# A wider first piece for a pooling kernel: 1500 columns on partitions 0 to 74 instead of 840 on 0 to 29

## Chip, cores, metric

One core of one Trainium2 chip. The metric is the device time of one execution in microseconds (us). Every execution is listed with its span too, the time from the first to the last instruction in the trace; for the kernel before the device time is 1.74 to 1.83 us longer than the span. All executions here are of the fast state with a granted clock of 1.00, but for one kernel that ran only once, whose state is unknown for that reason.

Terms: DVE is the vector engine, ACT the scalar engine, SBUF the on-chip memory of 128 partitions. A load or store is spread over up to 16 DMA engines, which move it in packets, here one per row (what one partition holds of it). An engine that has done its share sends an increment to a semaphore; at the sixteenth the transfer has landed.

## The reference

```python
# x: (32, 256, 4096) float32, p = 2, kernel_size = 4
for i in range(out_length):                       # 1024
    window = np.abs(x[:, :, 4*i:4*i+4]) ** p
    result[:, :, i] = np.mean(window, axis=-1) ** (1.0 / p)
```

So each four neighbours give the square root of the mean of their squares. 134.22 MB are read and 33.55 MB written; nothing is reused.

## The kernel before

The input is taken as one flat array, seen as 128 partitions by 262,144 columns. 20 loads of up to 13,184 columns go through three buffers. ACT squares a load in place, DVE sums the fours, ACT takes the root, and the result is stored. Loads are issued from the sync queue, most stores from ACT's. Ahead of the first load comes a small "first piece" of the array's end, in another shape: 840 columns of the 128-partition view, laid on 30 partitions.

```python
    slots += [[(W, [5792, 7392])], [(10808, [6592, 2808, 1408])]]   # the last load
    ODD = 840
    ...
    Q = 30
    odd = ODD * P // Q                                  # 3584 columns on 30 partitions
    t = o_tiles[1][0:Q, 0:odd]
    nc.sync.dma_start(out=t, in_=xf[(total - ODD) * P:total * P].rearrange("(p w) -> p w", p=Q))
    ahead = 0
    while ahead < n and loads[ahead][0] < X_SLOTS:      # the first three loads
        load(ahead)
        ahead += 1
    nc.vector.tensor_tensor(out=t, in0=t, in1=t, op=mybir.AluOpType.mult)
    ...                                                 # reduce, root
    stores["odd"] = nc.scalar.dma_start(...)            # 30 rows of 896
    for i in range(n):                                  # the 20 loads
        ...                                             # load ahead, square, sum, root, store
    for g in sorted(late):
        store(g, nc.sync)                               # the last four stores
```

What the first piece is for: a transfer of 30 rows runs on 15 DMA engines, one of 128 rows on 16. So one engine has no part in the first piece and gets a little less to do than the others. Below it is called **the engine outside**, and the others **the 15**.

## Time and profile before

| | kernel before |
|---|---|
| device time at first, median of 3 executions | 393.83 us (393.81 to 395.14) |
| the same with all 6 executions of the first comparison | 394.30 us (393.63 to 395.37) |
| span of the profiled execution | 393.33 us |
| moved by the DMA engines | 167.77 MB, 427 GB/s over the span |
| DVE, ACT busy | 70%, 70% |

The lines are from the timeline of the profiled execution (start us, duration us, engine, line, operation, shapes, and in brackets the idle time of the engine before it and what ended it):

```profile
4.96 3.88 DVE L137 TENSOR_TENSOR ot<-ot 30x3584 f32<-30x3584 f32 x1 [4.96 <-DMA ot<-in_x_dram]
20.60 11.19 ACT L167 ACTIVATE xt<-xt 128x13184 f32<-128x13184 f32 x1 [6.87 <-DMA xt<-in_x_dram]
```

They serve as clocks for two landings: DVE can begin when the first piece has landed on its last engine (4.96 us), and ACT when the first load has (20.60 us).

### The profile page before, as it was taken

To read this page: it belongs to the slowest core of one execution; us is meant where nothing else is said; L and a number is where in the kernel's file an instruction comes from. 1 tells how busy PE (TensorE), PEld (TensorE's weight loads), DVE (VectorE), ACT (ScalarE), POOL (GpSimd) and SP (SyncE) were. 2 spreads that over 40 slices of the span, in tenths; PEclk is the share of its full clock that TensorE was granted. 3 is DMA by queue.
4 is the path that set the end of the run, shared out by engine and by line. 5 is a ranking of instruction groups with operands and counts; after the bars stand their busy time and mean duration, and the time that the engine had idled before them with its cause. 6 is when DMAs were issued, how large, how long until landed. Compare 5 with 4: busy or idle time off the path is not lost.

```text
span 393.3 us, 182 instructions
## 1 busy us (share of the span) xinstructions
DVE 274.5 (70%) x36; ACT 275.4 (70%) x38; POOL 0.2 (0%) x4
## 2 busy tenths in 40 slices
DVE  4207898885869376948693869396929690989991
ACT  1095879919990899099809991998099809986991
POOL 0000000000000000000000000000000000000000
DMA  8999999999989999999999999999999899999996
GB/s 312 429 440 429 467 445 451 381 432 469 434 386 429 472 429 429 456 402 429 429 432 426 429 472 429 456 400 467 429 437 429 386 429 467 429 429 423 440 409 295
DMA packets 4554, 167.77 MB, mean 427 GB/s; under 512 B 526, under 2 KB 526, under 8 KB 556
## 3 DMA queue, kind: packets, MB, share of 16 engines
q1 hardware_dynamic: 3501, 144.04, 85.0%
q10 hardware_dynamic: 1053, 23.73, 14.0%
HBM read 134.22 MB, written 33.55 MB: 427 GB/s over the span
## 4 chain that ended last, share of the span: by engine, by line
DMA 54%; ACT 25%; DVE 19%; SPq 0%; issue 0%; ACTq 0%
DMA xt<-in_x_dram 54%; ACT xt L167 22%; DVE ot L111 14%; DVE xt L122 3%; ACT ot L102 3%; DVE ot L124 1%; DVE xt L124 1%; ACT xt L102 1%; SPq L82 0%; ACTq L99 0%; SPq L132 0%
## 5 line engine op out<-in xcount | busy, mean ns | idle before, releaser
L167 ACT ACTIVATE xt<-xt 128x13184 f32<-128x13184 f32 (+4 forms) x23 | 217.4, 9458 | 97.9 <-DMA xt<-in_x_dram 96.2
L111 DVE TENSOR_REDUCE ot<-xt 128x3296 f32<-128x13184 f32 x15 | 208.3, 13886 | 88.7 <-ACT xt L167 88.7
L102 ACT ACTIVATE ot<-ot 128x6592 f32<-128x6592 f32 x9 | 51.1, 5679 | 0.0
L122 DVE TENSOR_TENSOR xt<-xt 128x3296 f32<-128x3296 f32 (+5 forms) x9 | 34.5, 3834 | 16.9 <-ACT xt L167 16.8
L124 DVE TENSOR_TENSOR ot<-xt 128x3296 f32<-128x3296 f32 (+1 forms) x4 | 10.9, 2733 | 0.1
L143 ACT ACTIVATE ot<-ot 30x896 f32<-30x896 f32 x1 | 0.9, 948 | 10.8 <-DVE ot L139 10.8
L137 DVE TENSOR_TENSOR ot<-ot 30x3584 f32<-30x3584 f32 x1 | 3.9, 3880 | 5.0 <-DMA ot<-in_x_dram 5.0
L124 DVE TENSOR_TENSOR xt<-xt 128x1448 f32<-128x1448 f32 (+4 forms) x5 | 7.0, 1409 | 0.2
L102 ACT ACTIVATE xt<-xt 128x3296 f32<-128x3296 f32 (+3 forms) x4 | 5.8, 1445 | 1.1 <-DVE xt L124 1.1
L164 DVE TENSOR_TENSOR xt<-xt 128x5792 f32<-128x5792 f32 x1 | 6.2, 6184 | 0.0
L139 DVE TENSOR_REDUCE ot<-ot 30x896 f32<-30x3584 f32 x1 | 3.9, 3874 | 0.0
L143 ACT ACT_TABLE_LOAD x1 | 1.3, 1283 | 0.7 <-PEq L200 0.7
L200 POOL MEMSET const-bfloat16-1.0<- 128x1 bf16 x1 | 0.1, 101 | 0.0
L200 POOL MEMSET const-uint8-127<- 128x1 uint8 x1 | 0.1, 101 | 0.0
L200 POOL MEMSET const-float32-0.0<- 128x1 f32 x1 | 0.1, 98 | 0.2 <-issue 0.2
L200 POOL MEMSET const-float32-1.0<- 128x1 f32 x1 | 0.1, 98 | 0.0
## 6 DMA issues: line engine op xcount, KB each, us to landing
xt<-in_x_dram SPq DMA_DIRECT2D x19, 6592.0 KB, 31.6
out_dram<-ot ACTq DMA_DIRECT2D x7, 3296.0 KB, 27.4
out_dram<-ot SPq DMA_DIRECT2D x2, 3296.0 KB, 24.0
xt<-in_x_dram SPq DMA_DIRECT2D x1, 5404.0 KB, 24.1
out_dram<-xt SPq DMA_DIRECT2D x1, 1648.0 KB, 11.0
out_dram<-xt SPq DMA_DIRECT2D x1, 1351.0 KB, 6.6
ot<-in_x_dram SPq DMA_DIRECT2D x1, 420.0 KB, 4.2
out_dram<-ot ACTq DMA_DIRECT2D x1, 105.0 KB, 8.7
```

The source lines that it names most:

```text
L102: r = nc.scalar.activation(out=o, in_=o, func=Act.Sqrt, scale=1.0 / k)
L111: r = nc.vector.tensor_reduce(out=o, in_=v.rearrange("p (n j) -> p n j", j=k), axis=mybir.AxisListType.X, op=add,)
L122: r = nc.vector.tensor_tensor(out=h, in0=q[:, :, 0:2], in1=q[:, :, 2:4], op=add)
L124: r = nc.vector.tensor_tensor(out=o, in0=h[:, :, 0], in1=h[:, :, 1], op=add)
L137: nc.vector.tensor_tensor(out=t, in0=t, in1=t, op=mybir.AluOpType.mult)
L139: nc.vector.tensor_reduce(out=o, in_=t.rearrange("p (n j) -> p n j", j=k), axis=mybir.AxisListType.X, op=mybir.AluOpType.add,)
L143: nc.scalar.activation(out=o, in_=o, func=Act.Sqrt, scale=1.0 / k)
L164: r = nc.vector.tensor_tensor(out=v, in0=v, in1=v, op=mybir.AluOpType.mult)
L167: r = nc.scalar.activation(out=v, in_=v, func=Act.Square)
L200: nc = _bacc.Bacc("TRN2", target_bir_lowering=False, num_devices=1)
```

## The change

The intent: give the engine outside still less to do than the 15, by a wider first piece (1500 columns, and 660 fewer in the last load). 1500 columns on 30 partitions would be 6400 wide plus 1600 for the sums, more than the buffer's 6592, so the piece goes on 75 partitions (5 rows for each of 15 engines), 2560 wide.

```diff
-    slots += [[(W, [5792, 7392])], [(10808, [6592, 2808, 1408])]]
-    ODD = 840
+    slots += [[(W, [5792, 7392])], [(10148, [6440, 2456, 1252])]]
+    ODD = 1500
...
-    Q = 30
+    LOW, Q, PARTS = 0, 75, [(0, 75)]
     odd = ODD * P // Q
...
+    pieces = [(wide[a:b, 0:odd], wide[a:b, odd:odd + odd // k]) for a, b in PARTS]
+    for t, _ in pieces:
+        nc.vector.tensor_tensor(out=t, in0=t, in1=t, op=mybir.AluOpType.mult)
...                          # the reduction and the root in such loops too (one pass here)
```

More of the change, by code (lines that the diff above doesn't have):

```diff
@@ L126, in total_sum @@
         sums.append(r)
-    Q = 30
+    LOW, Q, PARTS = 0, 75, [(0, 75)]
     odd = ODD * P // Q
-    t = o_tiles[1][0:Q, 0:odd]
-    nc.sync.dma_start(out=t, in_=xf[(total - ODD) * P:total * P].rearrange("(p w) -> p w", p=Q))
+    wide = o_tiles[1]
+    nc.sync.dma_start(
+        out=wide[LOW:LOW + Q, 0:odd],
+        in_=xf[(total - ODD) * P:total * P].rearrange("(p w) -> p w", p=Q),
+    )
     ahead = 0
@@ L136 @@
         ahead += 1
-    nc.vector.tensor_tensor(out=t, in0=t, in1=t, op=mybir.AluOpType.mult)
-    o = o_tiles[1][0:Q, odd:odd + odd // k]
-    nc.vector.tensor_reduce(
-        out=o, in_=t.rearrange("p (n j) -> p n j", j=k),
-        axis=mybir.AxisListType.X, op=mybir.AluOpType.add,
-    )
-    nc.scalar.activation(out=o, in_=o, func=Act.Sqrt, scale=1.0 / k)
+    pieces = [(wide[a:b, 0:odd], wide[a:b, odd:odd + odd // k]) for a, b in PARTS]
+    for t, _ in pieces:
+        nc.vector.tensor_tensor(out=t, in0=t, in1=t, op=mybir.AluOpType.mult)
+    for t, o in pieces:
+        nc.vector.tensor_reduce(
+            out=o, in_=t.rearrange("p (n j) -> p n j", j=k),
+            axis=mybir.AxisListType.X, op=mybir.AluOpType.add,
+        )
+    for _, o in pieces:
+        nc.scalar.activation(out=o, in_=o, func=Act.Sqrt, scale=1.0 / k)
     stores["odd"] = nc.scalar.dma_start(
-        out=of[(total - ODD) * P // k:total * P // k].rearrange("(p w) -> p w", p=Q), in_=o,
+        out=of[(total - ODD) * P // k:total * P // k].rearrange("(p w) -> p w", p=Q),
+        in_=wide[LOW:LOW + Q, odd:odd + odd // k],
     )
```

## The prediction

> **What bounds the kernel now.** I read the page of the kernel before from the top: busy strips, totals of the DMA queues, chain of work that ended last.
>
> ```profile
> DVE  4207898885869376948693869396929690989991
> ACT  1095879919990899099809991998099809986991
> DMA  8999999999989999999999999999999899999996
> HBM read 134.22 MB, written 33.55 MB: 427 GB/s over the span
> DMA 54%; ACT 25%; DVE 19%; SPq 0%; issue 0%; ACTq 0%
> ```
>
> The two compute engines are busy 70% each and have gaps everywhere; the DMA strip is full except in the first and the last slice. The chain goes through ACT and DVE for 44% of the span, which suggests that compute matters. It is the path by which buffers come free, and the next views show that they come free early enough. The windows view (microseconds, busy time of DVE, ACT and POOL, TensorE clock, DMA share, GB/s):
>
> ```profile
> 0.00:10.00 10.00, 5.00 (x2) 1.28 (x1) 0.20 (x4) 1.00 0.92 349
> 10.00:50.00 40.00, 19.23 (x3) 23.33 (x3) 0.00 (x0) 1.00 1.00 432
> 200.00:300.00 100.00, 69.19 (x6) 71.28 (x8) 0.00 (x0) 1.00 1.00 434
> 370.00:394.00 24.00, 14.56 (x8) 14.76 (x7) 0.00 (x0) 1.00 0.84 359
> ```
>
> From 10 us on the engines move 432 to 434 GB/s at a share of 1.00. The critical list shows a refill asked for long before the queue needs it:
>
> ```profile
> 80.20 13.90 DVE ot L111
> 94.10 0.02 issue
> 94.11 34.89 DMA xt<-in_x_dram
> ```
>
> That load takes 34.89 us although its eight rows per DMA engine need 8 x 1.95 = 15.6 us: it stands in a queue that is never empty. I then strung the single packet records together into 16 engines, each packet joined to the one that ended as it began. A packet of 52,736 B takes 1,947 ns, of 26,368 B 978 ns, of 10,808 B 406 ns: about 9 ns plus 0.03675 ns per byte (27.2 GB/s per engine). No engine has a gap over 40 ns after 10 us. So the end is set by bytes per DMA engine, and by the latest of the 16 engines.
>
> Which is latest? The engine that takes no part in the first piece ends its last packet at 392.09 us, the other 15 at 390.23 to 390.60. The completion increments agree (sorted, us from the start, first two and last two of sixteen):
>
> ```
> first piece      1.30  4.40 ...   4.82   4.94
> load landing 3rd 51.05 51.38 ... 51.72  51.73
> load at 129      128.43 128.45 ... 128.73 129.00
> load at 262      261.73 261.78 ... 261.96 262.20
> load at 323      322.08 322.09 ... 322.35 323.66
> last store       390.73 390.88 ... 391.09 392.54
> ```
>
> One engine is first by 0.33 us up to 51 us, last by about 0.25 us from 106 to 301 us, and last by 1.3 to 1.6 us from 323 us. Its packets lost 0.82 us at 72 us and 1.35 us between 304 and 324 us, compared with their nominal times; no other engine lost more than 0.44 us in all after 10 us. Since the total of bytes stays, the change can act only on this imbalance.
>
> **What the Trainium skill says.** First, "DMA: Bandwidth & Descriptors", section "Why a DMA increments its semaphore by 16 and not by 1": the number of engines is the largest up to 16 that divides the outer dimension of both sides, and the sequencer writes the missing increments at once. So 30 and 75 rows both give 15 engines (2 and 5 rows each), and 128 rows 16. The trace agrees: of the first piece's sixteen increments one comes at 1.30 us, the other 15 at 4.40 to 4.94. Second, the same page's "Where 436 GB/s comes from" puts the ceiling at 435.2 GB/s; the trace has 432 to 434 in steady stretches. Third, "SBUF — State Buffer", section "Door 1: The DMA port swizzle": partitions p and p+32 share a port, p+64 has another. Partitions 0 to 29 reach 8 of 16 ports, 0 to 74 reach 11. The trace fits: the 30 first packets of 14,336 B took a median 907 ns where the line above gives 536. Fourth, "DMA: Bandwidth & Descriptors", "Latency and other measured facts": engines 7 and 15 are usually slower, with a guess that has to do with DMAs issued from GpSimd. This kernel issues none there, yet one engine is slower by its 2.4 us of lost time; the guess is not supported here.
>
> **The change, part by part.** The instruction order on every engine stays; only widths differ.
>
> Engine 16, outside the first piece: the last load shrinks from 10,808 to 10,148 columns, 8 rows x 2,640 B less: 21,120 x 0.03675 = 776 ns. The last store shrinks by 8 x 660 B: 194 ns. Sum: 0.97 us less. Nothing is added.
>
> The other 15: the same 0.97 us less at the end. At the start, 2 packets of 14,336 B (2 x 536 = 1,072 ns) become 5 of 10,240 B (5 x 385 = 1,925): +0.85 us. The piece's store, 2 packets of 3,584 B (2 x 140 = 280 ns), becomes 5 of 2,560 B (5 x 103 = 515): +0.23 us. Sum 1.08 - 0.97 = +0.11 us. If the ports set the first piece's pace, 4 rows per port (4 x 536 = 2.14 us) become 8 (8 x 385 = 3.08): +0.94 instead of +0.85, so +0.20 us.
>
> Compute: the square and the reduction of the first piece take 3.88 and 3.87 us for 3,584 columns; at 2,560 that is about 2.8 each, so 2.2 us less on DVE. It ends at 12.75 us now, and the first large load lands at 20.6, so this is worth nothing. The first ACT square slips with its load by up to 0.9 us; the fourth load is then asked for at 46.9 instead of 46.0 us, still some 4 us before the queue would drain at 51 to 52. At the end the last square is issued earlier and its pieces are 2 to 12% shorter; the last store is ready about 1.5 us earlier. It was already ready first: issued at 385.92, while the engines reach its packets at 387.1 (388.9 on the late one).
>
> So in the profiled execution the late engine ends at 392.09 - 0.97 = 391.12 and the others at up to 390.60 + 0.20 = 390.8: the late one still ends last, and the span falls by 0.97 us, to 392.36.
>
> **Two kinds of execution.** The timed runs are 395.14, 393.83 and 393.81 us, and the profiled execution is listed with 395.11. I take it that 395.1 are those with the late 1.35 us of lost time and 393.8 those without. A check: without it the late engine would keep its earlier 0.25 us lag and finish 1.54 - 0.25 = 1.29 us sooner: 395.11 - 1.29 = 393.82, as measured. This is inferred; only one execution has a trace. In the quick kind the late engine has only 0.25 us to give, and then the others bind, 0.11 to 0.20 later: 393.82 - 0.25 + 0.20 = 393.77. In the slow kind: 395.12 - 0.97 = 394.15. The median should be that of the quick kind, with some chance of the slow one: **393.9 us**.
>
> **Rivals.** (a) The lost time at 304 to 324 us is in every execution and 395.1 is an offset of profiling. For it: lost time always on one engine. Against: 395.14 without a profile. Then the median falls by 0.97, to 392.9. (b) The low partitions serialise more than counted: 13 of the 15 engines write 8 ports, in an uneven order, and the first piece costs not 0.94 but up to 1.5 us more. For it: 907 ns against 536. Against: engines that share a port now still lose only part of it, since the start has latency to hide it in. Then the 15 engines become the bound and the time rises to about 394.3. (c) A buffer comes free too late after the later start, and the queue runs dry. Margin of some 4 us against a shift of 0.9: unlikely, and it would cost under 1 us. (d) The tail's compute becomes the bound since the DMA ends earlier: excluded by the 1.2 us of readiness, which grows.
>
> **Range and chances.** The cases span 392.9 (a) to 394.3 (b). I hold (a) for less likely, one in six, because the arithmetic of the two kinds closes to 0.02 us, so it does not move the middle, but the range takes in both ends: 392.8 to 394.4 for 8 in 10, the rest mostly above, for a first piece that costs more than (b). A 2% change is 7.9 us; nothing that the change touches is that large (its whole added transfer is under 3 us even at half speed). So 98.5% for within 2%.
>
> **What would show each step.** One increment of the first piece again at about 1.3 us and 15 later ones, about 0.9 us later than 4.94. The late engine ahead of the others by about 1.3 us at 51 us (0.33 now), by about 0.8 at 262 us (0.25 behind now), and within 0.5 us of them at the last store. The last load's packets 40,592 B at about 1.50 us. Wrong would be: the 15 engines ending over 0.5 us after the one; gaps in the DMA strip before 370 us; or a first piece landing after 6.5 us.

## The result, and the profile after

| device time, us | kernel before | changed kernel |
|---|---|---|
| first comparison, median (6 executions each) | 394.30 (393.63 to 395.37) | 394.46 (394.24 to 394.94) |
| repeated with more rounds, median (11 and 6) | 393.93 (393.66 to 395.09) | 394.54 (394.45 to 394.63) |
| ratio, first comparison | | 1.0002 (95% interval 0.9983 to 1.0020) |
| ratio, repeated | | 1.0006 (0.9989 to 1.0023) |

A ratio is the mean time of one kernel's fast runs over that of the other's of the same rounds, so it is not quite the ratio of the medians. The single executions say more. Those of the repeat, sorted:

```
before:  393.66 393.68 393.81 393.83 393.89 393.93 | 394.93 395.03 395.06 395.08 395.09
changed: 394.45 394.51 394.54 394.54 394.58 394.63
```

The kernel before has two kinds of execution, a quick one (mean of the six: 393.80) and a slow one (mean of the five: 395.04). The changed kernel has one group (mean 394.54) between them: 0.74 us above the quick kind and 0.50 us below the slow one. Nearly equal means hide two opposite effects. How they balance depends on the mix: of all 35 executions of the kernel before, 22 are quick (up to 394.03), 11 slow (from 394.93) and two lie between (394.34, 394.78), so their median is 393.91 and their mean 394.29. Against the 12 of the changed kernel (mean 394.52) that is more often a loss of 0.6 us than a gain of 0.5. All this is far below the 2% of the verdict and also below the 0.3% within which executions usually agree (1.2 us), so it is read from groups of executions and from traces, of which each kernel has one.

From the timeline of the changed kernel, the same two clocks:

```profile
6.82 2.82 DVE L143 TENSOR_TENSOR ot<-ot 75x2560 f32<-75x2560 f32 x1 [6.82 <-DMA ot<-in_x_dram]
22.44 11.19 ACT L175 ACTIVATE xt<-xt 128x13184 f32<-128x13184 f32 x1 [9.18 <-DMA xt<-in_x_dram]
```

The first piece lands 1.86 us later (6.82 instead of 4.96) and the first load 1.84 us later; some 0.9 had been predicted. DVE's two instructions on the piece are shorter (2.82 instead of 3.88 us), as predicted, and it does not matter. The page and the windows view of the changed kernel (window, length, busy time of DVE, ACT, POOL, TensorE clock, DMA share, GB/s):

```profile
DMA  9999999989999999999989999999999999999997
HBM read 134.22 MB, written 33.55 MB: 427 GB/s over the span
```

```profile
0.00:10.00 10.00, 3.14 (x2) 1.28 (x1) 0.20 (x4) 1.00 0.94 330
200.00:300.00 100.00, 69.05 (x6) 69.38 (x8) 0.00 (x0) 1.00 1.00 431
370.00:394.00 24.00, 14.65 (x8) 14.18 (x7) 0.00 (x0) 1.00 0.87 372
```

The DMA strip is as full as before, so nothing ran dry. In the first 10 us it moved 330 GB/s, where the kernel before moved 349, although its share of busy time rose from 0.92 to 0.94: the engines were occupied and slow. In the last 24 us it is the other way round, 372 against 359, at a share of 0.87 against 0.84: the 16 engines now end closer together.

The completion increments of single transfers show where the time went (from the trace's records, us from the start; first of the sixteen, median, last; the control is the changed kernel run again):

```
                     before                  changed                 changed, control
first piece          4.40*   4.58   4.94     5.84*   6.06   6.80     5.70*   5.95   6.47
first load          19.90   20.42  20.58    21.10   21.97  22.42    20.99   21.90  22.16
fourth load         66.64   67.16  67.32    67.87   68.92  69.34    67.75   68.82  69.09
last store         390.73  390.98 392.54   391.36  391.77 392.37   390.56  391.50 391.96
* the first that a DMA engine sent; at 1.30 us comes the one that the sequencer writes at once
```

The median stands for the 15. They are 1.55 us later at the first load (1.48 in the control) and 0.79 us later at the last store (0.52). That is nearly the sum: 1.55 for the start, plus 0.23 for the piece's store as the prediction works it out, less 0.97 for the shorter end, is 0.81 (0.74 in the control, which measured 0.52). About 0.1 of the 0.23 is counted twice, since 53 of the store's 75 packets had already run when the first load landed, and all 30 in the kernel before. If in the quick kind of the kernel before the engine outside ends about with the 15, as the prediction infers (no quick execution of it has a trace), a quick execution pays this in full, and 0.74 us is what it paid. This last step is inferred. In the profiled execution of the kernel before the engine outside ended 1.45 us behind the next (391.09 to 392.54). In the control it ends 0.7 us ahead of the next (390.56; it is the first from the first load on), so the 15 set the end there.

### The profile page after: what moved, and what is told of

Same layout as the page of the kernel before. It is cut to its first block, busy times and chain, and to the rows that moved or that the text cites. A ratio compares the mean times of both kernels' runs of the same rounds, so it can differ in the third digit from the quotient of the medians.

```text
span 393.2 us, 181 instructions
## 1 busy us (share of the span) xinstructions
DVE 271.7 (69%) x36; ACT 274.6 (70%) x38; POOL 0.2 (0%) x4
## 4 chain that ended last, share of the span: by engine, by line
DMA 44%; ACT 31%; DVE 21%; another core or an unknown queue 1%; issue 1%; ACTq 0%; SPq 0%
DMA xt<-in_x_dram 44%; ACT xt L175 26%; DVE ot L111 14%; ACT ot L102 4%; DVE xt L122 4%; DVE xt L172 2%; DVE xt L124 1%; ACT xt L102 1%; DVE ot L124 0%; ACTq L99 0%; SPq L133 0%; SPq L82 0%
## 5 line engine op out<-in xcount | busy, mean ns | idle before, releaser
L175 ACT ACTIVATE xt<-xt 128x13184 f32<-128x13184 f32 (+5 forms) x23 | 216.9, 9435 | 98.3 <-DMA xt<-in_x_dram 96.6
L122 DVE TENSOR_TENSOR xt<-xt 128x6592 f32<-128x6592 f32 (+6 forms) x9 | 34.2, 3795 | 15.6 <-ACT xt L175 15.5
L143 DVE TENSOR_TENSOR ot<-ot 75x2560 f32<-75x2560 f32 x1 | 2.8, 2822 | 6.8 <-DMA ot<-in_x_dram 6.8
L145 DVE TENSOR_REDUCE ot<-ot 75x640 f32<-75x2560 f32 x1 | 2.8, 2817 | 0.0
## 6 DMA issues: line engine op xcount, KB each, us to landing
out_dram<-ot ACTq DMA_DIRECT2D x7, 3296.0 KB, 27.2
```

Of the source, the lines that this page charges most:

```text
L122: r = nc.vector.tensor_tensor(out=h, in0=q[:, :, 0:2], in1=q[:, :, 2:4], op=add)
L145: nc.vector.tensor_reduce(out=o, in_=t.rearrange("p (n j) -> p n j", j=k), axis=mybir.AxisListType.X, op=mybir.AluOpType.add,)
L175: r = nc.scalar.activation(out=v, in_=v, func=Act.Square)
```

## The experiments

What was open: why did the wider piece cost the 15 engines 1.5 us at the start rather than 0.9? Theory: several engines write one port of SBUF at a time. Rivals: the bytes or the number of descriptors as such; a slow start of the memory. Further: why is the engine outside late as well, and is there a placement or width that wins? The kernels differ from the changed kernel in the edit shown and, where the width differs, in the last load. All results were correct, and by the 2% rule every kernel is "the same" as the kernel before (the one that ran once has no verdict). Times are device time in us; "piece done" is the end of the last packet of the first piece in the trace, and it starts at 1.72 to 1.76 in all of these kernels.

### 60 rows on partitions 0 to 59

```diff
-    LOW, Q, PARTS = 0, 75, [(0, 75)]
+    LOW, Q, PARTS = 0, 60, [(0, 60)]
```

> The same 1500 columns as 60 rows of 12,800 B on partitions 0 to 59 (15 engines, 4 rows each). Port theory (the low partitions reach few ports, and the first piece goes at the pace of the fullest one): 8 rows of 12,800 B per port, 3.84 us at 479 ns a packet, where 75 rows had 3.08 and took 3.66 to 3.96 in fact; so the last packet of the first piece ends at about 6.3 us (5.70 with 75 rows), the others land the first load at about 22.6 us and the last store 0.5 to 0.8 us later than with 75 rows; time about 395.0. Rival (the start costs by bytes or by descriptors, not by place): same bytes and fewer descriptors, first piece ends at 5.3 to 5.7 us, the same as q60_mid; time 394.4.

Measured: piece done at 5.75 us, the first load's median at 22.20, the last store's median 392.31, 0.54 later than in the changed kernel. Time 394.91 (394.75 to 395.02), ratio 1.0020 (1.0002 to 1.0039). The piece was done 0.55 us sooner than the port theory had it, hardly later than with 75 rows (5.70), and the load 0.4 sooner (22.6 expected); the last store and the time fit it, and the time is about 0.5 above the rival's.

### The same 60 rows on partitions 32 to 91

```diff
+    LOW, Q, PARTS = 32, 60, [(32, 64), (64, 92)]
```

> The same 60 rows of 12,800 B on partitions 32 to 91, so that by the page on SBUF no port gets over 4 rows. Port theory: the engine limit 4 x 479 ns = 1.9 us plus some 0.6 of start, last packet of the first piece at 4.2 to 4.5 us (5.70 before), the other engines land the first load at about 20.8 us (21.97 median before), the last store 1.2 us earlier (390.6), and then the engine outside the first piece ends last again by 0.5 to 1.5 us; time 393.3 to 394.2. Rival: no different from q60_low, the first piece ends at 5.3 to 5.7 us; time 394.4.

(The page meant is the Trainium skill's "SBUF — State Buffer", section "Door 1: The DMA port swizzle".) From section 6 of the page (DMA issue, KB, us from issue to landing), first on partitions 0 to 59, then on 32 to 91:

```profile
ot<-in_x_dram SPq DMA_DIRECT2D x1, 750.0 KB, 5.9
```

```profile
ot<-in_x_dram SPq DMA_DIRECT2D x1, 750.0 KB, 4.3
```

Same bytes, same rows, same number of descriptors, only another place: 1.6 us. Piece done at 4.67 us instead of 5.75, the first load's median at 20.33 instead of 22.20. So place decides, and neither the bytes nor the descriptors. The single packets say the same: the median packet of the piece took 481 ns on partitions 32 to 91, which is the nominal time of 12,800 B by the prediction's line (479), and 980 ns on 0 to 59. But the last store's median is 391.15, not the 390.6 predicted, the engine that ends last is 0.12 us behind the next and not 0.5 to 1.5, and the time is 394.45 (394.20 to 395.27), ratio 1.0013 (0.9991 to 1.0034): no gain. Part of that is outside the span. Time less span is 2.05 us here (394.20 and 392.15) and 1.79 with 60 rows on low partitions; see the single-instruction kernel below.

### 75 rows on partitions 32 to 106

```diff
+    LOW, Q, PARTS = 32, 75, [(32, 64), (64, 107)]
```

> The change's 75 rows of 10,240 B moved to partitions 32 to 106 alone. Port theory: most ports get 4 rows, two or three get 7 or 8; most engines are done by 4.5 us, the last ones at 4.8 to 5.3; last store of the others 0.7 to 1.0 us earlier than in the changed kernel; time 393.4 to 394.2. Rival (bytes or descriptors at the start): as in the changed kernel, 5.4 to 5.7 us and 394.4.

Piece done at 5.26 us for the last engine, at 4.88 for the median of the 15 (5.27 in the changed kernel). The last engine is where it was expected; of the others most were expected by 4.5. The last store's median is 391.34, 0.43 sooner than in the changed kernel, where 0.7 to 1.0 was expected. Time 394.49 (394.41 to 394.61), ratio 1.0010 (0.9992 to 1.0029), above the 393.4 to 394.2 of the port theory.

### The old width on 60 middle rows

```diff
+    LOW, Q, PARTS = 32, 60, [(32, 64), (64, 92)]        # with ODD = 840
```

> The width of the kernel before (840), but as 60 rows of 7,168 B on partitions 32 to 91. Port theory: 4 x 272 ns = 1.1 us at most per engine and per port, so the first piece ends at about 3.3 us (3.92 before) and the others land the first load at about 19.9 us instead of 20.4. The other engines gain 0.4 us at the end, but the one outside has as much to do as before and ends last by 0.6 to 2 us: time as before, 393.6 to 395.2. Rival: first piece ends at 3.9 us, as before.

Piece done at 3.44 us (3.92 in the kernel before), first load's median 19.61 (20.42). So the kernel before pays for shared ports as well. The packets took 272 ns, the nominal time, where the kernel before has 907 for nominal 536. Last store's median 391.14, against 390.98 before: the 0.8 us of the first load were gone by then. Time 395.06 (394.31 to 395.77) with two of four executions above 395.5; ratio 1.0031 (1.0005 to 1.0056).

### Control: the changed kernel again

> The changed kernel itself, unchanged, as a control in the same rounds. If my reading of two kinds of execution is right, the kernel before shows executions near 393.8 and near 395.2 us, and this one a single group: the 15 engines, late from the start, end last in nearly all of them. 394.2 to 394.6 us, at most one in five near 395.3; ratio to before within 0.999 to 1.002.

394.54 (394.45 to 394.63), one group beside the two of the kernel before. The expectation held; the numbers are in the result above.

### 120 rows on partitions 0 to 119

```diff
+    LOW, Q, PARTS = 0, 120, [(0, 120)]
```

> The same 1500 columns as 120 rows of 6,400 B on partitions 0 to 119: 15 engines with 8 rows each, all 16 ports with 4 to 8 rows, and one compute instruction of each kind (the 60-row and 75-row kernels on middle partitions need two, and show 2.05 us outside the span where the others show 1.78). Port theory: 8 x 244 ns = 1.95 us for the fullest port and the engine, so the last packet of the first piece ends at 4.4 to 4.8 us as with 60 rows on the middle partitions (4.68), in spite of the most descriptors of all; the other engines land the first load at about 20.4 us. Rival (number of descriptors): 120 rows are slower than 75 on low partitions, over 5.7 us. Time 393.8 to 394.3 (0.2 to 0.5 below the changed kernel).

This missed. Piece done at 5.58 us, not 4.4 to 4.8, although the piece reaches all 16 ports; time 394.59 (394.48 to 394.94), ratio 1.0008 (0.9993 to 1.0023). The rival expected over 5.7. So "how many ports are reached" and "how many rows per port" both fail as the measure. What the theory lacked, I think, is time: each engine takes its rows in order. Suppose that with 8 rows each, engine e writes partitions 8e to 8e+7, four of them behind one port and four behind the next, and engine e+4 (32 partitions on) is at the same port at the same moment. Then at any time 15 engines are at 8 ports. (Which engine takes which rows is an assumption; the records do not name the engine.) I worked this out for every placement: each engine takes its rows in turn at 27.2 GB/s, and engines at one port at the same time share that rate. The port of a partition is from the Trainium skill, "SBUF — State Buffer", section "Door 1: The DMA port swizzle". No start-up time is included. Against it stands what was measured, less the 1.74 us at which the piece starts. "Last" is the end of the piece's last packet; the measured median is that of the times at which the 15 begin on the first load (all engines but the one that begins first):

```
                                 worked out              measured
                                 median    last          median    last
before    30 rows, 0 to 29        2.11     2.11           1.87     2.18
old width 60 rows, 32 to 91       1.05     1.05           1.59     1.70
changed   75 rows, 0 to 74        3.01     3.39           3.53     3.96
          75 rows, 32 to 106      1.88     3.39           3.14     3.52
          60 rows, 0 to 59        3.76     3.76           3.73     4.01
          60 rows, 32 to 91       1.88     1.88           2.57     2.93
          120 rows, 0 to 119      3.76     3.76           3.51     3.84
1200      120 rows, 0 to 119      3.01     3.01           2.48     3.42   (next section)
```

Where no port is shared, 0.5 to 1.0 us of start-up shows; where ports are shared it is partly hidden. With 1500 columns the one placement without shared ports is done in 2.9 us and the others in 3.5 to 4.0. The model was made after these results and is rough: the median of the 75 rows on 32 to 106 lies far above it (3.14 against 1.88), and that of the 1200 columns in 120 rows below it (2.48 against 3.01), although no start-up is included. That engines at one port at the same moment slow each other is thus likely, not shown. The packet times exclude the rival of the descriptors more firmly than the ends do. A row of 10,240 B took 385 ns (median) as one of 60 on partitions 32 to 91, 595 as one of 75 on 32 to 106 and 685 as one of 75 on 0 to 74, where its nominal time is 385; with 120 rows, 6,400 B took 444 (nominal 244). The packets themselves are slowed, by a factor of up to two, and no fixed cost for each explains this.

### 1200 columns in 120 rows

```diff
+    ODD = 1200      # last load 10448: 6520, 2620, 1308
+    LOW, Q, PARTS = 0, 120, [(0, 120)]
```

> As q120_1500 with 1200 columns (1,280 a row). First piece 8 x 197 = 1.58 us, ends at 4.0 to 4.4 us. The other 15 engines are late by less at the start and shorter by less at the end, so end as in q120_1500 within 0.2 us; the engine outside has 0.44 us more to do. If its lost time is what makes the slow executions, the quick ones are at 393.6 to 394.0 and the slow ones at 394.6 to 395.0; median 393.9.

394.33 (394.15 to 394.89): four executions at 394.15 to 394.43 and two at 394.86 and 394.89, ratio 1.0004 (0.9988 to 1.0020). Piece done at 5.16 us, not 4.0 to 4.4: the same miss as with 1500. The median was expected at 393.9. Two kinds of execution appear again, the quick one (mean 394.25) 0.45 us above that of the kernel before.

### The first piece from another queue

```diff
-    nc.sync.dma_start(
+    nc.scalar.dma_start(
         out=wide[LOW:LOW + Q, 0:odd],
```

> The changed kernel with the first piece issued from the ACT queue instead of the sync queue. The engine that takes no part in the first piece began its first load packet at 3.56 us and ended it at 7.07 (2.86 and 5.62 in the kernel before), and at 7.04 to 7.19 in all three other 1500-column placements. Theory (its descriptors are made behind those of the first piece on the same queue, so that queue's order holds it back): from another queue its packet ends by about 4.8 to 5.4 us and it leads the others by 1.7 us or more at the first load's landing (0.6 to 0.9 in the changed kernel). Rival (the memory or the engines' start is slow for all, whatever the queue): 7.0 us again. The time is set by the other 15 engines, on the same ports: 394.2 to 394.7 in both cases.

399.26 (399.05 to 399.63), ratio 1.0127 (1.0107 to 1.0146): 4.7 us slower than the control, which no theory had. The timeline and the windows of this kernel:

```profile
21.40 2.82 DVE L143 TENSOR_TENSOR ot<-ot 75x2560 f32<-75x2560 f32 x1 [21.40 <-DMA ot<-in_x_dram]
```

```profile
0.00:10.00 10.00, 0.00 (x0) 1.28 (x1) 0.20 (x4) 1.00 0.89 289
10.00:20.00 10.00, 0.00 (x0) 0.00 (x0) 0.00 (x0) 1.00 1.00 320
```

and the same second window of the control:

```profile
10.00:20.00 10.00, 2.16 (x1) 0.74 (x1) 0.00 (x0) 1.00 0.99 429
```

From two queues every engine goes to and fro between packets of the first load and of the first piece. Five of the latter per engine are spread over the time from 4.2 to 18.8 us, each aimed at a port that may be another engine's at that moment; the load's packets of 52,736 B mostly take 2.4 to 2.9 us up to about 19 us, instead of 1.95. The engines are busy (share 1.00) at 320 GB/s. The piece lands at 21.40 us, and ACT, which takes its root first, begins on the first load at 28.3 us. Whether this is the port conflict again, stretched over 15 us instead of 4, is not shown, and the size speaks against ports shared evenly as the whole of it: by even sharing, five packets per engine of nominally 0.385 us could hold up the others by at most 1.9 us per engine, but its seven or so slow load packets lost some 0.65 us each, 4.5 in all. The piece on clear partitions from ACT's queue was not tried. As to the engine outside, the trial leans to the theory: all 16 engines ended their first load packet by 5.74 us, and the first increment of the first load (22.62) leads the median by 1.95 us. It is not clean, since everything else moved as well, and 5.74 is above the 4.8 to 5.4 expected of that engine.

### 60 rows on partitions 64 to 123

```diff
+    LOW, Q, PARTS = 64, 60, [(64, 124)]
```

> 1500 columns as 60 rows on partitions 64 to 123. Theory as it stands after the runs so far: what counts is how many of the 15 engines write one port at the same time, row by row; two at once here (engines e and e+8 are 32 partitions apart), as on partitions 0 to 59, so the last packet of the first piece ends at about 1.74 + 3.76 = 5.5 to 5.8 us. Rival (it is the low partitions that are slow): as on the middle partitions, 4.2 to 4.7 us.

```profile
ot<-in_x_dram SPq DMA_DIRECT2D x1, 750.0 KB, 6.0
```

As on partitions 0 to 59 (5.9), and not as on 32 to 91 (4.3). The last packet ended at 6.10 us, 0.3 above the range, with a median of 5.60. The packets took 968 ns, as there (980; nominal 479). So low partitions are not slow as such. It does not test the model against the count of ports: this placement reaches 8 ports, as 0 to 59 does, and 32 to 91 reaches 15. One execution, 395.07.

### 60 middle rows, computed by single instructions

```diff
+    LOW, Q, PARTS = 32, 60, [(0, 92)]
+    nc.gpsimd.memset(wide[0:LOW, 0:odd], 0.0)
```

> 60 rows on partitions 32 to 91, each engine with a port of its own, but computed by single instructions over partitions 0 to 91 with the unused rows set to zero first. First piece ends at 4.3 to 4.7 us as with two compute instructions. If those caused the 0.27 us outside the span, time minus span is 1.75 to 1.80 again, and the time is 394.45 - 0.27 = 394.2 (393.9 to 394.4), below the changed kernel's 394.5; if not, 394.4 to 394.5.

Time less span is 1.75 to 1.82 us, so the 0.27 us outside the span came with the split into two DVE instructions more and one ACT instruction more. It is no price per instruction: the kernel without a first piece, below, has two DVE instructions and one of ACT fewer than the kernel before, and the same 1.78 us (395.60 and 393.82). What it is stays open. But the time is 394.67 (394.15 to 395.58), ratio 1.0015 (0.9999 to 1.0032): not better than the changed kernel. Where did the good start go? Medians of the increments, this kernel less the control:

```
first load    fourth load   load at 107   load at 146   load at 168   last store
  -1.02          -0.96         -0.39         -0.39         -0.09         -0.04
```

The lead of a full microsecond holds for the first four loads, falls to 0.4 when the first large stores come between 70 and 96 us, and is gone by 168 us. Packet by packet, the 16 engines of this kernel lose 0.9 to 2.7 us in all against the nominal packet times after 10 us, much of it at 71, 74 and 150 us; in the control 15 engines lost nothing over the 0.03 us that I count from. This is why the kernels with a good start gained so little: it is given back later. That it happens is measured in one execution per kernel, and that of this kernel was its slowest (395.58); the other 60-row kernel on middle partitions shows half of it in its quickest (394.20): 1.64 us ahead of the changed kernel at the first load, 0.71 at 107 us, 0.62 at the last store. Why an evenly started set of engines loses more there is not settled.

### The same with 1200 columns

> The same with 1200 columns: first piece ends at 1.74 + 1.51 + 0.6 = 3.9 us. The engine outside starts sooner than with 1500 and has 0.44 us more to do. The candidate for the best: median 393.6 to 394.1, quick executions near 393.6, slow ones near 394.8. Rival (what is won at the start is lost when the first large store comes, as 0.5 us of it was with 60 rows and 1500 columns): 393.9 to 394.3, no better than the kernel before.

395.01 (393.92 to 395.30), ratio 1.0014 (0.9997 to 1.0031): two executions at 393.92 and 393.94, four at 394.90 to 395.30. Piece done at 4.54 us, not 3.9. Neither expectation fits the median. The quick ones are where the quick ones of the kernel before are (393.80 to 394.03 in these rounds). This was the candidate for the best; no kernel of this study beats the kernel before.

### No first piece

```diff
-    ODD = 840       # edited from the kernel before
+    ODD = 0         # last load 11648: 7104, 3024, 1520; the code of the piece cut out
```

> No first piece: all 16 engines move the same. Theory: the sixteenth engine gets 0.97 x 840/660 = 1.24 us more to do than in the kernel before but starts 1.1 us sooner, so that it ends last by about the same; the others are spared the shared ports (0.5 us). Quick executions 393.8 to 394.2, slow ones 395.2 to 395.6, in about the proportion of the kernel before. Rival (the first piece is what balances the engines): every execution is slow, 395 or more.

395.63 (395.17 to 396.17), ratio 1.0037 (1.0016 to 1.0058): every execution is slow, as the rival said; but its reason, that the first piece is what balances the engines, is not shown. The first load's increments begin at 18.29 us and end at 19.27 us; the spread of a load then grows to 2.31 us (367.61 to 369.92, the last load; 1.78 in the kernel before). In this kernel too one engine lags, though none is outside. But the tail shows another cost. First the kernel before, then this one (first square of the last load, last root, last store):

```profile
369.77 5.70 ACT L167 ACTIVATE xt<-xt 128x6592 f32<-128x6592 f32 x1 [0.83 <-DMA xt<-in_x_dram]
385.40 0.50 ACT L102 ACTIVATE xt<-xt 128x352 f32<-128x352 f32 x1 [0.84 <-DVE xt L124]
385.92 0.33 SPq L99 DMA_DIRECT2D out_dram<-xt  x1
```

```profile
369.94 6.12 ACT L154 ACTIVATE xt<-xt 128x7104 f32<-128x7104 f32 x1 [1.82 <-DMA xt<-in_x_dram]
386.68 0.52 ACT L102 ACTIVATE xt<-xt 128x380 f32<-128x380 f32 x1 [0.88 <-DVE xt L124]
387.23 0.33 SPq L99 DMA_DIRECT2D out_dram<-xt  x1
```

The last store is issued at 387.23 us; the increments of the store before begin at 387.13, so for most engines the queue has run dry by then: they end the store ahead from 386.8 us on and begin the last one at 388.06. In the kernel before the last issue is at 385.92, and the last store begins at 386.99 as the store ahead ends: no gap. The last load lands only 0.17 us later than in the kernel before (369.92 against 369.75), but its 840 columns more take 1.1 us more of squares, sums and roots (17.3 us from landing to issue against 16.2). So it is mainly the wider last load that makes the last store late, by 1.0 us for the median engine (391.97 against 390.98), and this trial does not separate it from balance.

## Why the prediction was right or wrong

The time was inside the range, 0.6 above the point, and "no change of 2%" was safe from the size of the thing. The route to the number was in part wrong.

- **The bound** was right. The DMA engines' bytes and the latest engine set the end in both kernels; DVE's 2.1 us less, the later first squares and the shorter tail pieces changed nothing, and nothing ran dry. Two readings were too smooth: "432 to 434 GB/s" from 10 us on holds for the windows shown, while all windows from 10 to 370 us lie at 423 to 448; and the last store was issued at 385.88 us, not 1.5 us before 385.92, since the last load landed no earlier. The margin of 1.2 us left out the time from issue to the first packet, 0.83 us in the kernel without a first piece (387.23 to 388.06).
- **15 engines for 75 rows** was right: one increment at 1.30 us, 15 from 5.84 us on. The last load's packets of 40,592 B took 1.50 us, as worked out.
- **Two kinds of execution** were right: the repeat has six executions at 393.7 to 393.9 and five at 394.9 to 395.1 of the kernel before. Rival (a), that all are slow, falls. The traces of the other kernels bear out what makes them: in slow executions (395.11 of the kernel before, 395.58 and 394.86 of 60 single-instruction rows with 1500 and 120 rows with 1200 columns) the last increment comes 1.45, 1.25 and 0.86 us behind the next, in quick ones (394.31 of the old width, 394.20 of 60 middle rows, 393.92 of single instructions with 1200 columns) at most 0.12.
- **The step that failed: the first piece's cost for the 15**, "+0.85", or "+0.94" with ports. It measured 1.66 us where the 15 begin on the first load (median engine; 1.78 for the last) and 1.5 at the first load's landing. The trials tell the parts: on partitions 32 to 91, where the packets kept their nominal time, the step from 840 to 1500 columns cost 0.98 us (median, 1.59 to 2.57), near the 0.85 for the bytes; the other 0.68 came with the place, for which the sum had 0.09. (One trace each, and the numbers of rows differ.) Rival (b) named this, with up to 1.5 us more. The sum with ports took the fullest port, 2.14 us before and 3.08 after; measured were 1.87 and 3.53, so it was too high for the one and too low for the other. Worked out by the engines at one port at the same time it is 2.11 us before and 3.01 to 3.39 after, 0.9 to 1.3 more, so that model does not explain the miss either: 0.5 to 0.8 us remain open.
- **The engine outside: "Nothing is added"** was wrong. It began its first load packet at 3.56 us (4.03 in the control) instead of 2.86, ended it at 7.07 (6.90) instead of 5.62, and landed the first load at 21.10 instead of 19.90. The shorter end of 0.97 is thus more than used up by 1.1 to 1.2 us of a later start. With 1500 columns that packet, taken to be the first load packet to start, ends at 6.90 to 7.22 us in all placements with the sync queue; with 1200 at 6.23 to 6.55. So it goes with the size of the piece, not with its place. The order of descriptors on one queue is likely, not shown. So this engine led the next by 0.9 us at the third load, where 1.3 had been predicted. Two of the prediction's own signs of being wrong came true: the first piece landed after 6.5 us (6.82; 6.49 in the control), and in the control the 15 ended 0.7 to 1.4 us after the one.
- **The quick kind: 393.77 predicted, 394.5 measured.** It follows from the two: the 15 end 0.5 to 0.8 us later, not 0.11 to 0.20.
- **The slow kind: 394.15 predicted, none seen** in 12 executions, the highest 394.94. By the account above an engine outside that lost 2.4 us, as in the profiled execution before, would end near 392.54 + 1.2 - 0.97 = 392.8 at the last store, above every increment seen. It lost less in the executions that have a trace: in the changed kernel its lead of 0.9 us shrinks to 0.1 between 146 and 186 us, in the control it keeps 0.7. The kernels whose engine outside runs clearly ahead after the start (changed, control, 60 low rows, 75 middle rows, 120 rows with 1500 columns) have two executions above the rest among 26, both at 394.94; those in which all run more abreast have more (60 middle rows 1 of 4, the old width 2 of 4, single instructions 2 of 6 and 4 of 6, 120 rows with 1200 columns 2 of 6). What the lost time is, and why it depends on this, is open.
- **The sum**: the change takes about 0.5 us from the slow kind and adds 0.74 to the quick one, so the mean moves by only 0.2. That the median came near the point is due to the small sizes of all terms, not to the sum that gave 393.9: that one had the 15 pay 0.11 to 0.20, and was lucky to lie within 0.6.

## What to carry to other kernels

A transfer that uses fewer rows than 128 should be tried on several partition ranges: the same 60 rows took 4.3 us on partitions 32 to 91, 5.9 on 0 to 59 and 6.0 on 64 to 123. Compare the time of its packets with that of like ones that run alone; where it is doubled, engines are likely to be at one SBUF port at the same moment. A helper transfer that balances the DMA engines has a price of its own at the start, and here it grew faster than the bytes moved; what it gains was not isolated (leaving it out also made the tail longer). Look at single executions before believing a mean: here a nearly unchanged mean was one better and one worse kind of execution, and a good start was lost again at the first large stores.

## What the Trainium skill lacked or had wrong

- "SBUF — State Buffer", section "Door 1: The DMA port swizzle": it says that the bandwidth depends on how many of the 16 ports the partitions reach. 120 rows that reach all 16 were done at 5.58 us, hardly sooner than 60 rows that reach 8 (5.75), and 60 others, which reach 15, were done at 4.67. The ports in use at the same time agree with this order, but a working from the port map was off by up to 1.3 us for the median engine, so that this is the measure is not shown.
- "DMA: Bandwidth & Descriptors", section "Rules for kernel authors": issuing from several queues "Doesn't help" bandwidth. Here it hurt: issued from ACT's queue beside a load on the sync queue, the piece came with 320 GB/s instead of 429 between 10 and 20 us and cost 4.7 us.
- "DMA: Bandwidth & Descriptors", section "Latency and other measured facts": engines 7 and 15 are slower, as a best guess by DMAs issued from GpSimd. None is issued there here, and yet one engine lost 2.4 us in one execution of the kernel before. The traces do not number the engines.
- No page has it that an engine outside a transfer starts its part of the next one on the same queue later, the larger that transfer is: its first packet ended at 5.62 us behind 840 columns and at 6.90 to 7.22 behind 1500.
- No page has it that device time can grow outside the span: it was about 2.05 us longer than the span where the piece was computed by split instructions, and about 1.78 elsewhere, in the kernel with the fewest instructions too.
